# Attention of a two-layer decoder: causal masks added by matmuls, PSUM buffers divided anew, three value products split, divisions spread, late tokens first in the last head

## The chip, the cores and the metric

The kernel runs on one core of one Trainium2 chip. The metric is the device time of one execution in microseconds (us); the median of several runs counts. Engines are named as in the profile: PE is TensorE (PEld its weight loads), DVE is VectorE, ACT is ScalarE, POOL is GpSimd, SP is SyncE, whose queue issues most DMA transfers.

## The reference

A decoder trunk of two layers over 1024 tokens with 1024 features. Layer 0 is multi-head latent attention with 12 heads, layer 1 sliding-window attention; each has four memory cross-attention heads beside it, an output projection and a squared-ReLU MLP. The change is in layer 0's attention and in its output projection. Cut to what matters:

```python
def causal_dense_attention(q, k, v):          # q, k: 96 wide, v: 64 wide, 12 heads
    ...
        sc = jnp.einsum('bqhd,bkhd->bhqk', q_blk, k,
                        preferred_element_type=jnp.float32) * scale
        mask = k_idx[None, :] <= t_idx[:, None]
        sc = jnp.where(mask[None, None], sc, NEG)
        p = jax.nn.softmax(sc, axis=-1).astype(v.dtype)
        return jnp.einsum('bhqk,bkhd->bqhd', p, v)
...
        x = x + jnp.concatenate([mix, cross], axis=-1) @ w_o[i]
```

Inputs and output are float32.

## The kernel before

**Number format.** Most products are made from split operands: a float32 value is copied by ScalarE into a rounded part `hi` (type fp32r) and VectorE subtracts to get `lo`. A product then takes three matmul passes: hi·hi, hi·lo, lo·hi (`mm3`, L97). A product of unsplit float32 operands is one call, and the profile shows it as two matmul records (x2). The profile prints fp32r operands of matmuls as f32.

**Scores and row maxima.** For each head, `head_tiles` (L678) brings the head's queries and keys together by four DMAs, and splits them: ScalarE makes `qh` and `kh`, GpSimd subtracts for `ql` and `kl`. The softmax needs each query's largest score. `row_max(h, i)` (L707) makes the rough scores of query tile i against all keys up to its own tile (one pass, hi·hi) in a two-bank PSUM buffer (`ps2`, psx). VectorE then reduces the columns ahead of the diagonal tile (L718), and a second VectorE instruction adds the causal mask `dmask` to the diagonal 128 columns and takes the maximum (L719). `max_row` (L694) transposes the eight maxima and writes them, split, as row 96 of `qh` and `ql`, so that the score matmuls subtract them.

`scores(h, G, k)` (L815) makes transposed scores: keys of tile k on the partitions, queries of half G (512 tokens) on the columns, three passes over 97 rows into a one-bank buffer (`ps1`, pss). On the diagonal (k >= 4G) only the columns from the diagonal on are made (512, 384, 256 or 128), and VectorE adds `dmaskT` to the first 128 columns (L825). ScalarE takes the exponential into `p` (L827). For the early half (G = 0) `p` is split into `ph` and `pl`; the blocks of G = 1 stay whole (`WHOLE`).

**Values.** `values(h, G, k)` (L836) adds a block to the output pso of that half: one unsplit product of `vf` and `p` for G = 1 (L846), three passes for G = 0 (L849, L850 with 64 columns of weights, L854; that of the first block is issued last, L856). The weights have 64 columns of ones beside the 64 of v, so rows 64 to 127 hold the softmax denominators.

**Order.** The 12 blocks of a head are walked in the fixed list `blocks`, alternating the halves; step n issues the scores of block n and the values of block n - 2 (`LV = 2`). The row maxima of the next head are put between them by the table `ahead`, and `v_tiles` and `head_tiles` at steps 6 and 2 of a head. The framework then plans each engine's instruction order from this written order, its priorities and its own estimate of times, so an instruction can run ahead of its written place: the first split of w_o, written at step 4 of head 10, runs in the trace at 431.78 us, in head 9.

**Divisions.** Of heads 0 to 10 the undivided output goes by DMA into `qn`, and the denominators into `den`. `rc_split(c)` takes the reciprocals of a batch of heads (6 and 5), splits them and puts them in two rows per head by DMA; `rc_mul(c)` (L886) spreads each over 64 partitions by two matmuls of 6 or 5 rows with the selector `sel` (psrc, L894 and L895), and VectorE multiplies `qn` with it (L897). A batch's `rc_mul` is issued in one piece. The last head is divided directly: reciprocal of 64 x 512 (L859) and a product (L861) for each half.

**PSUM.** One pool for the whole kernel: two buffers of two banks (tag s) and four of one bank (tag m).

**Output projection.** `wo_phase` (L1015) goes over the eight token tiles twice, once for each half of w_o's columns, in the order `TORD` = 0, 4, 1, 5, 2, 6, 3, 7. Each tile's attention output is split by `o_split` (part 0 is `f0`, heads 0 to 7; part 1 is `f1`, heads 8 to 11 and the cross heads), and 24 matmuls follow (pswo).

Of the kernel before, what the change touches and what calls it, by code (L numbers as in the profile page):

```python
# [55 lines left out]
def trunk(  # L56
# [19 lines left out]
    ps_pool = pool("psum", space=PSUM)  # L76
    dram = ctx.enter_context(tc.tile_pool(name="dram", bufs=1, space=DRAM))

    def ps2(name):
        return ps_pool.tile([P, 1024], F32, tag="s", bufs=2, name=name)  # L80

    def ps1(name):
        return ps_pool.tile([P, 512], F32, tag="m", bufs=4, name=name)
# [34 lines left out]
    dmask = const.tile([P, P], F32, name="dmask")  # L118
    nc.gpsimd.memset(dmask, 0.0)
    nc.gpsimd.affine_select(out=dmask, in_=dmask, compare_op=ALU.is_ge, fill=NEG, base=0, pattern=[[-1, P]], channel_multiplier=1)  # L120
    dmaskT = const.tile([P, P], F32, name="dmaskT")
    nc.gpsimd.memset(dmaskT, 0.0)
    nc.gpsimd.affine_select(out=dmaskT, in_=dmaskT, compare_op=ALU.is_ge, fill=NEG, base=0, pattern=[[1, P]], channel_multiplier=-1)
# [342 lines left out]
    rope_tables()  # L466
    mem_kv(0, kv0, memT, pm)
# [239 lines left out]
    def row_max(h, i):  # L707
        if h not in m8s:
            m8s[h] = hb.tile([P, NT], F32, tag="m8", bufs=2, name=f"m8_{h}")
        qh, ql, kh, kl = bufs_[h % 3]  # L710
        n = (i + 1) * P
        ps = ps2(f"psx{h}_{i}")
        for a in range(0, n, 512):
            b = min(a + 512, n)
            nc.tensor.matmul(ps[:, a:b], qh[0:96, i * P : (i + 1) * P], kh[0:96, a:b], start=True, stop=True)  # L715
        m = m8s[h][:, i : i + 1]
        if i:
            nc.vector.reduce_max(m, ps[:, : n - P], axis=AX, negate=True)  # L718
        nc.vector.tensor_tensor_reduce(ps[:, n - P : n], ps[:, n - P : n], dmask, -1.0, m if i else -NEG, ALU.add, ALU.min, accum_out=m)  # L719
# [72 lines left out]

    at = pool("at", "right")
    for i in (1, 2):
        head_bufs(at, i)
# [16 lines left out]
    WHOLE = {(1, k) for k in range(8)}  # L812
    probs, po_ = {}, {}

    def scores(h, G, k):  # L815
        qh, ql, kh, kl = bufs_[h % 3]
        c0 = max(0, k - 4 * G) * P
        ks = slice(k * P, (k + 1) * P)
        qs = slice(G * 512 + c0, G * 512 + 512)
        ps = ps1(f"pss{h}_{G}_{k}")[:, c0:]  # L820
        nc.tensor.matmul(ps, kh[:, ks], qh[:, qs], start=True, stop=False)  # L821
        nc.tensor.matmul(ps, kh[:, ks], ql[:, qs], start=False, stop=False)
        nc.tensor.matmul(ps, kl[:, ks], qh[:, qs], start=False, stop=True)
        if k >= 4 * G:
            nc.vector.tensor_tensor(ps[:, 0:P], ps[:, 0:P], dmaskT, ALU.add)  # L825
        p = at.tile([P, 512], F32, tag="p", bufs=5, name=f"p{h}_{G}_{k}")
        nc.scalar.activation(p[:, c0:], ps, AF.Exp, scale=SC)  # L827
        if (G, k) in WHOLE:
            probs[(h, G, k)] = (p,)
            return  # L830
        ph = at.tile([P, 512], F32R, tag="ph", bufs=3, name=f"ph{h}_{G}_{k}")
        pl = at.tile([P, 512], F32R, tag="pl", bufs=3, name=f"pl{h}_{G}_{k}")
        split(p[:, c0:], ph[:, c0:], pl[:, c0:])
        probs[(h, G, k)] = (ph, pl)

    def values(h, G, k):  # L836
        vh, vl, vf = vbufs[h % 2]
        c0 = max(0, k - 4 * G) * P
# [5 lines left out]
        pr = probs.pop((h, G, k))  # L844
        if len(pr) == 1:
            nc.tensor.matmul(po[:, c0:], vf[:, k, :], pr[0][:, c0:], start=first, stop=last)  # L846
        else:
            ph, pl = pr
            nc.tensor.matmul(po[:, c0:], vh[:, k, :], ph[:, c0:], start=first, stop=False)  # L849
            nc.tensor.matmul(po[0:64, c0:], vl[:, k, :], ph[:, c0:], start=False, stop=False)  # L850
            if first and G == 0:
                probs["late"] = pl
            else:
                nc.tensor.matmul(po[:, c0:], vh[:, k, :], pl[:, c0:], start=False, stop=last and G == 1)  # L854
            if last and G == 0:
                nc.tensor.matmul(po, vh[:, 0, :], probs.pop("late"), start=False, stop=True)  # L856
        if last and h == H - 1:
            tmp = at.tile([64, 512], F32, tag="on", bufs=2, name=f"rq{h}_{G}")
            nc.vector.reciprocal(tmp, po[64:128])  # L859
            r = slice((h % 2) * 64, (h % 2) * 64 + 64)  # L860
            nc.vector.tensor_tensor(qn[h // 2][r, G * 512 : (G + 1) * 512], po[0:64], tmp, ALU.mult)  # L861
        elif last:
            on = at.tile([65, 512], F32, tag="on", bufs=2, name=f"on{h}_{G}")
            nc.scalar.activation(on, po[0:65], AF.Copy)
            r = slice((h % 2) * 64, (h % 2) * 64 + 64)
            nc.sync.dma_start(out=qn[h // 2][r, G * 512 : (G + 1) * 512], in_=on[0:64])
            d0 = (h % 6) * NT + 4 * G
            nc.sync.dma_start(out=den[h // 6][d0 : d0 + 4, :], in_=on[64:65])

    den = [at.tile([n, P], F32, name=f"den{n}") for n in (48, 40)]  # L870
# [3 lines left out]
    def rc_split(c):  # L874

        n = (6, 5)[c] * NT
# [9 lines left out]
    def rc_mul(c):  # L886
        rT = r_tiles.pop(c)
        n = (6, 5)[c]
        for s in halves:
            for j in range((n + 1) // 2):  # L890
# [5 lines left out]
                o = qn[3 * c + j][0 : 64 * m, s]  # L896
                nc.vector.tensor_tensor(o, pb, o, ALU.mult)  # L897

# [4 lines left out]
    seq = [(h,) + b for h in range(H) for b in blocks]  # L903

    ahead = {}
    for h in range(1, H):
        for i, d in ((7, -3), (6, -2), (5, -1), (4, 0), (3, 1), (2, 3), (1, 5), (0, 6), (8, 7)) if h > 1 else ((7, 3), (6, 4), (5, 5), (4, 6), (3, 7), (2, 8), (1, 9), (0, 9), (8, 10)):
            ahead.setdefault((h - 1) * len(blocks) + d, []).append((h, i))
    for n in range(len(seq) + LV):
        if n < len(seq):  # L910
            h, G, k = seq[n]
            j = n % len(blocks)
            scores(h, G, k)
            for g, i in ahead.get(n, ()):
                if i < NT:
                    row_max(g, i)
                else:
                    max_row(g)
            if h + 1 < H and j == 6:
                v_tiles(h + 1)  # L920
            if j == 2 and h + 2 < H:
                head_tiles(h + 2)
        if n >= LV:
            values(*seq[n - LV])
        if n >= 10 * len(blocks) and n % 2 == 0:
            wq.step()
        if n == 5 * len(blocks) + 3:
# [3 lines left out]
        if n == 5 * len(blocks) + 10:  # L931
            nc.scalar.activation(sel, sel32, AF.Copy)
        if n == 6 * len(blocks) + LV + 3:
            rc_split(0)
        if n == 7 * len(blocks) + LV:
            rc_mul(0)
        if n == 11 * len(blocks) + LV + 1:
            rc_split(1)
        if n == 11 * len(blocks) + LV + 8:
            rc_mul(1)  # L940
    at.release()
    hb.release()
# [72 lines left out]
    def wo_phase(layer, wq, o, m):  # L1015
# [12 lines left out]
        def o_split(t, parts_=(0, 1)):  # L1028
            r = []
            for i in parts_:  # L1030
                d = m.t(f"d{oct_[0] % 3}", F32R)
                oct_[0] += 1
                oh, ol = k4(d[:, 0, :]), k4(d[:, 1, :])
                split(o[i][:, :, t * P : (t + 1) * P], oh, ol)
                r += [(oh[:, k, :], ol[:, k, :]) for k in range(4)]
            return r

# [4 lines left out]

# [797 lines left out]
```

## Time and profile before

| | |
|---|---|
| median of 3 runs | 2184.77 us (2184.66 to 2185.63) |
| the profiled execution | 2188.77 us, its span 2187.1 us |
| mean granted TensorE clock | 0.988 |
| first score matmul of layer 0's attention | 254.38 us |
| third matmul of the output projection | 490.64 us |

The span is what the profile's times count in; the profiled execution's own time has 1.7 us around it. A row of the timeline gives start, duration, engine, line, operation, output <- inputs, and in brackets how long the engine was idle before and who released it. A row by windows gives the busy time of each engine with the number of instructions, then TensorE's granted clock (1.00 is full speed), the DMA engines' share and GB/s. A row by groups gives line, engine, operation, tiles and shapes, count | busy us, mean ns | idle before it and the releasers.

### The profile page before, as it was taken

How to read it: one execution, taken by the hardware profiler on the slowest of the kernel's cores; microseconds unless marked ns; L12 is line 12 of the kernel's file. 1: busy time of each engine (PE TensorE's matmuls, PEld its weight loads, DVE VectorE, ACT ScalarE, POOL GpSimd, SP SyncE). 2: the span in 40 equal slices, each digit the busy share in tenths (PEclk: the TensorE clock that was granted, in tenths of full speed). 3: DMA queues.
4: the chain of work that ended last, by engine and by line, in shares of the span. 5: the costliest groups of instructions: out<-in, count | busy, mean ns of one | idle time of the engine just before them, and what ended most of it. 6: DMA issues, size and time to landing. Idle time of an engine off the chain costs nothing.

```text
span 2187.1 us, 28756 instructions
## 1 busy us (share of the span) xinstructions
PE 2129.5 (97%) x9781; PEld 1715.1 (78%) x9781; DVE 1491.2 (68%) x3026; ACT 1000.9 (46%) x2119; POOL 234.4 (11%) x263
## 2 busy tenths in 40 slices
PE   6999999999999999999999999999999999999998
PEld 5888776658788888888888788668788888788887
DVE  6555677664997776786657443665987776785665
ACT  5455366544633333444445453774633333444452
POOL 0013433300000000000001133440000000000000
PEclk9999999899999999999999999999999999999999
DMA  7102222323254445953433111123254445854442
GB/s 245 59 11 59 52 69 46 80 88 121 83 173 150 140 141 175 342 198 125 164 118 99 63 39 49 39 76 108 78 175 148 159 158 176 319 189 139 131 121 87
DMA packets 171219, 272.97 MB, mean 125 GB/s; under 512 B 15699, under 2 KB 71744, under 8 KB 171072
## 3 DMA queue, kind: packets, MB, share of 16 engines
q1 hardware_dynamic: 164214, 253.80, 36.0%
q0 software_dynamic: 4016, 13.12, 1.6%
q10 hardware_dynamic: 2842, 4.22, 0.6%
q8 instruction: 77, 1.26, 0.2%
q14 instruction: 70, 0.57, 0.1%
HBM read 181.69 MB, written 76.81 MB: 118 GB/s over the span
## 4 chain that ended last, share of the span: by engine, by line
PE 87%; DVE 6%; ACT 2%; DMA 2%; issue 1%; POOL 1%; DVEq 0%; SPq 0%; ACTq 0%; POOLq 0%
PE psu L1214 5%; PE psu L1215 5%; PE psy L1501 5%; PE psy L1499 5%; PE psy L1500 5%; PE psu L1213 5%; PE psz L1499 4%; PE psz L1500 4%; PE psz L1501 4%; PE psv L1215 4%; PE psv L1214 4%; PE psv L1213 4%; PE pso L846 3%; PE pswo L102 2%; PE pswo L100 2%; PE pswo L101 2%
## 5 line engine op out<-in xcount | busy, mean ns | idle before, releaser
L91 ACT ACTIVATE i<-mr 128x512 fp32r<-128x512 f32 x78 | 49.3, 632 | 123.6 <-PE psu L1214 38.0
L827 ACT ACTIVATE p<-pss 128x512 f32<-128x512 f32 (+2 forms) x144 | 69.0, 484 | 77.4 <-DVE pss L825 55.7
L1499 PE MATMUL psy<-g 128*128 128x512 f32 x256 | 100.0, 391 | 0.0
L1500 PE MATMUL psy<-g 128*128 128x512 f32 x256 | 99.7, 390 | 0.0
L1501 PE MATMUL psy<-g 128*128 128x512 f32 x256 | 99.5, 390 | 0.0
L91 ACT ACTIVATE g<-i 128x512 fp32r<-128x512 f32 x79 | 49.7, 629 | 93.2 <-PE psz L1500 46.5
L846 PE MATMUL pso<-p,vf 128*128 128x512 f32 (+2 forms) x192 | 88.0, 542 | 0.7 <-ACT p L827 0.7
L92 DVE TENSOR_TENSOR g<-i,g 128x512 fp32r<-128x512 f32 x79 | 55.4, 702 | 45.9 <-ACT g L91 45.9
L821 PE MATMUL pss<-qh,kh 97*128 97x512 f32 (+2 forms) x144 | 77.8, 545 | 3.1 <-ACT p L827 2.5
L91 ACT ACTIVATE uh<-i 128x512 fp32r<-128x512 f32 x66 | 41.6, 630 | 83.5 <-PE psy L1500 40.7
L1499 PE MATMUL psz<-g 128*128 128x512 f32 x192 | 74.8, 389 | 0.0
L1501 PE MATMUL psz<-g 128*128 128x512 f32 x192 | 74.8, 389 | 0.0
L1500 PE MATMUL psz<-g 128*128 128x512 f32 x192 | 74.8, 389 | 0.0
L92 DVE TENSOR_TENSOR uh<-i,uh 128x512 fp32r<-128x512 f32 x66 | 45.6, 691 | 40.0 <-ACT uh L91 39.8
L718 DVE TENSOR_REDUCE m<-psx 128x1 f32<-128x128 f32 (+6 forms) x84 | 57.2, 686 | 20.7 <-PE psx L715 19.9
L92 DVE TENSOR_TENSOR i<-mr,i 128x512 fp32r<-128x512 f32 x78 | 53.8, 689 | 23.6 <-ACT i L91 23.4
L1424 DVE TENSOR_TENSOR mqf<-mqq,mqf 128x512 f32<-128x512 f32 x64 | 43.3, 690 | 28.8 <-DMA mqq<-in_mlp_w_down_dram 28.6
L1601 POOL TENSOR_TENSOR wsr<-wsr,gcol 128x1024 f32<-128x1024 f32 x12 | 23.7, 1979 | 352.7 <-DVE ul L1244 280.1
L91 ACT ACTIVATE i<-d 128x512 fp32r<-128x512 f32 x44 | 27.8, 633 | 70.2 <-PE psu L1214 39.6
L1501 PEld LDWEIGHTS psy<-g 128*128 128x128 f32 x256 | 48.1, 188 | 10.0
L1499 PEld LDWEIGHTS psy<-g 128*128 128x128 f32 x256 | 48.1, 188 | 9.8
L1500 PEld LDWEIGHTS psy<-g 128*128 128x128 f32 x256 | 48.1, 188 | 9.8
(610 smaller groups left out, 6942.2 us busy)
## 6 DMA issues: line engine op xcount, KB each, us to landing
i<-hd SPq DMA_DIRECT2D x154, 256.0 KB
hd<-uh SPq DMA_DIRECT2D x76, 256.0 KB
hd<-ul SPq DMA_DIRECT2D x76, 256.0 KB
mr<-in_mlp_w_up_dram SPq DMA_DIRECT2D x36, 512.0 KB
hd<-x SPq DMA_DIRECT2D x72, 256.0 KB
mr<-hd SPq DMA_DIRECT2D x70, 256.0 KB
d<-in_mlp_w_up_dram SPq DMA_DIRECT2D x32, 512.0 KB
mqq<-in_mlp_w_down_dram SPq DMA_DIRECT2D x32, 512.0 KB
```

The lines of the kernel that those rows point to most:

```text
L91: nc.scalar.activation(hi, src, AF.Copy)
L92: (lo_eng or nc.vector).tensor_tensor(lo, src, f32(hi), ALU.subtract)
L718: nc.vector.reduce_max(m, ps[:, : n - P], axis=AX, negate=True)
L821: nc.tensor.matmul(ps, kh[:, ks], qh[:, qs], start=True, stop=False)
L827: nc.scalar.activation(p[:, c0:], ps, AF.Exp, scale=SC)
L846: nc.tensor.matmul(po[:, c0:], vf[:, k, :], pr[0][:, c0:], start=first, stop=last)
L1213: nc.tensor.matmul(ps, wh[:, k, :], xh[:, k, :], start=p in (1, 2, 5) and k == 0, stop=False, skip_group_check=True)
L1214: nc.tensor.matmul(ps, wh[:, k, :], xl[:, k, :], start=False, stop=False, skip_group_check=True)
L1215: nc.tensor.matmul(ps, wl[:, k, :], xh[:, k, :], start=False, stop=k == 3, skip_group_check=True)
L1499: nc.tensor.matmul(ps, ah[:, j, :], bh, start=p in (1, 5, 2) and k == 0, stop=False, skip_group_check=True)
L1500: nc.tensor.matmul(ps, ah[:, j, :], bl, start=False, stop=False, skip_group_check=True)
L1501: nc.tensor.matmul(ps, al[:, j, :], bh, start=False, stop=k == NP - 1, skip_group_check=True)
```

## The change

1. *Masks.* An identity, `dmask` and `dmaskT` are bf16 tiles. The mask is added in PSUM by a matmul of the identity with the mask over the 128 diagonal columns, in `scores` after the first pass and in `row_max` as the last matmul. One reduction over all columns takes the row maximum.
2. *PSUM.* For the attention and the output projection of layer 0 the pool is released and made anew: six one-bank buffers and one two-bank buffer (tag x). Row maxima of tiles 0 to 3 use the former, of tiles 4 to 7 the latter. After the projection the old division returns.
3. *Value products.* (1, 1), (1, 2) and (1, 3) are split and take three passes; the early half's first block has its third pass in place. In the last head the early half stays whole.
4. *Order.* `scores` and `values` return lists of matmuls and a closure for what follows. Where either block is 128 columns wide, the two lists are issued alternately. The table `ahead` is shifted a little.
5. *Divisions.* Batches of 6, 4 and 1 heads; `rc_mul` is a generator that issues one pair of heads and one half in a step, late half first.
6. *Last head and projection.* The last head makes all late blocks and then the early ones; the late half is divided at once (`last_o(1)`), the early half inside the projection's second tile (`last_o(0)`). The projection's first pass goes over the tiles 4 to 7, then 0 to 3, with its split operands in the four x tiles; these lie where the key and query buffers of heads 10 and 11 were (pool hb1).

The core of the diff:

```diff
     def ps1(name):
-        return ps_pool.tile([P, 512], F32, tag="m", bufs=4, name=name)
+        return psum[0].tile([P, 512], F32, tag="m", bufs=4 if len(psum) == 1 else 6, name=name)
+    def psx(name):
+        return ps2(name) if len(psum) == 1 else psum[0].tile([P, 1024], F32, tag="x", bufs=1, name=name)
+    def new_psum(n):
+        psum[0].release()
+        psum[:] = [pool(f"psum{n}", space=PSUM)] * (2 if n == 1 else 1)
...
+    identb, dmask, dmaskT = [const.tile([P, P], BF16, name=n) for n in ("identb", "dmask", "dmaskT")]
+    def masks(pl):
+        nc.vector.tensor_copy(identb, ident)
+        for dst, sgn in ((dmask, 1), (dmaskT, -1)):
+            m = pl.tile([P, P], F32, tag="mask", bufs=2, name=f"mask{sgn}")
+            nc.gpsimd.memset(m, 0.0)
+            nc.gpsimd.affine_select(out=m, in_=m, compare_op=ALU.is_ge, fill=NEG, ...)
+            nc.vector.tensor_copy(dst, m)
...
     def row_max(h, i):
-        m = m8s[h][:, i : i + 1]
-        if i:
-            nc.vector.reduce_max(m, ps[:, : n - P], axis=AX, negate=True)
-        nc.vector.tensor_tensor_reduce(ps[:, n - P : n], ps[:, n - P : n], dmask, -1.0, m if i else -NEG, ALU.add, ALU.min, accum_out=m)
+        nc.tensor.matmul(ps[:, n - P : n], identb, dmask, start=False, stop=True, skip_group_check=True)
+        nc.vector.reduce_max(m8s[h][:, i : i + 1], ps[:, :n], axis=AX, negate=True)
...
+    blocks_end = [(1, k) for k in (0, 4, 5, 6, 7, 1, 2, 3)] + [(0, k) for k in range(4)]
-    WHOLE = {(1, k) for k in range(8)}
+    WHOLE = {(1, k) for k in (0, 4, 5, 6, 7)}
...
     def scores(h, G, k):
+        mms = [mm(ps, kh[:, ks], qh[:, qs], start=True, stop=False)]
+        if diag:
+            mms.append(mm(ps[:, 0:P], identb, dmaskT, start=False, stop=False))
+        mms.append(mm(ps, kh[:, ks], ql[:, qs], start=False, stop=False))
+        mms.append(mm(ps, kl[:, ks], qh[:, qs], start=False, stop=True))
...
-        if k >= 4 * G:
-            nc.vector.tensor_tensor(ps[:, 0:P], ps[:, 0:P], dmaskT, ALU.add)
...
+            if (G, k) in WHOLE or (h == H - 1 and G == 0):
+                probs[(h, G, k)] = (p,)
...
+    def last_o(G, tmp):
+        nc.vector.reciprocal(tmp, po_[G][64:128])
+        nc.vector.tensor_tensor(qn[5][64:128, G * 512 : (G + 1) * 512], po_[G][0:64], tmp, ALU.mult)
+    GRP = [0, 6, 10, 11]
...
     def rc_mul(c):
+        for s in halves[::-1]:
             for j in range((n + 1) // 2):
...
                 nc.vector.tensor_tensor(o, pb, o, ALU.mult)
+                yield
...
-        for i, d in ((7, -3), (6, -2), (5, -1), (4, 0), (3, 1), (2, 3), (1, 5), (0, 6), (8, 7)) if h > 1 else ...
+        for i, d in ((7, -4), (6, -2), (5, 0), (3, 1), (4, 2), (2, 3), (1, 5), (0, 6), (8, 7)) if h > 1 else ...
...
+        if ms and mv and P in (width(*seq[n][1:]), width(*seq[n - LV][1:])):
+            while ms and mv:
+                mix += [ms.pop(0), mv.pop(0)]
+        for f in mix + ms:
+            f()
...
+        next(muls, None)
...
+        if n == 7 * NB + LV:
+            muls = rc_mul(0)
+        if n == 10 * NB + LV + 1:
+            rc_split(1)
+        if n == 10 * NB + LV + 8:
+            muls = rc_mul(1)
+        if n == 11 * NB + LV + 1:
+            rc_split(2)
+        if n == 11 * NB + LV + 6:
+            muls = rc_mul(2)
...
     def wo_phase(layer, wq, o, m):
+        ORD = [[4, 5, 6, 7, 0, 1, 2, 3] if layer == 0 else TORD, TORD]
...
+                if p == 1 and layer == 0 and half == 0:
+                    last_o(0, m.t("i39")[0:64, 0, :])
```

199 lines of the change are left out of this document (111 added, 88 removed).

## The prediction

> **What bounds the kernel now.** First the page's busy line: TensorE is busy for 97% of the span, so only TensorE time counts, spent on matmuls, on waiting, or at a lowered clock.
>
> ```profile
> PE 2129.5 (97%) x9781; PEld 1715.1 (78%) x9781; DVE 1491.2 (68%) x3026; ACT 1000.9 (46%) x2119; POOL 234.4 (11%) x263
> ```
>
> The change touches only layer 0's attention and the start of its output projection. I cut that stretch at the first score matmul of each head (its start in the timeline), which gives heads 0 to 11, the last running to the output projection's third matmul, and a rest of 3.15 us. The columns are window, length, PE, PEld, DVE, ACT and POOL busy, granted clock, DMA.
>
> ```profile
> 254.38:278.33 23.95, 20.61 (x87) 14.68 (x87) 21.22 (x49) 13.12 (x25) 15.78 (x11) 0.93 0.29 65
> 278.33:293.42 15.09, 14.74 (x72) 10.99 (x71) 11.12 (x35) 10.38 (x21) 4.75 (x3) 1.00 0.39 84
> 293.42:310.13 16.71, 16.61 (x79) 12.29 (x78) 12.65 (x38) 11.22 (x23) 6.00 (x3) 1.00 0.27 64
> 310.13:326.86 16.73, 16.63 (x79) 12.28 (x78) 12.66 (x38) 11.12 (x23) 6.02 (x3) 1.00 0.27 64
> 326.86:343.57 16.71, 16.61 (x79) 12.28 (x78) 12.64 (x38) 11.15 (x23) 6.01 (x3) 1.00 0.29 64
> 343.57:362.26 18.69, 17.08 (x80) 12.13 (x78) 12.58 (x38) 11.26 (x24) 7.11 (x5) 1.00 0.26 57
> 362.26:379.23 16.97, 16.59 (x79) 12.25 (x78) 13.37 (x40) 11.07 (x24) 6.02 (x3) 1.00 0.09 21
> 379.23:407.52 28.29, 27.05 (x89) 17.59 (x88) 16.96 (x43) 10.82 (x22) 5.97 (x3) 0.78 0.24 58
> 407.52:427.67 20.15, 18.49 (x82) 12.73 (x80) 14.67 (x38) 10.84 (x23) 6.04 (x3) 0.97 0.29 65
> 427.67:446.08 18.41, 17.90 (x80) 12.35 (x78) 16.41 (x40) 14.26 (x26) 5.44 (x3) 1.00 0.50 153
> 446.08:461.50 15.42, 15.32 (x73) 11.25 (x72) 9.38 (x33) 8.57 (x19) 0.56 (x1) 1.00 0.19 52
> 461.50:490.64 29.14, 24.30 (x85) 13.78 (x83) 17.78 (x26) 11.95 (x24) 0.00 (x0) 0.88 0.29 91
> 490.64:493.79 3.15, 3.15 (x8) 2.48 (x8) 3.15 (x4) 0.00 (x0) 0.00 (x0) 0.50 0.02 5
> ```
>
> The reader is to see a steady head of 16.7 us with a full TensorE, and four places above it: head 0, heads 7 and 8, and the last head with what follows it. In the steady heads only TensorE work can be won or lost; in the other places there are waits and low clock.
>
> **TensorE's prices.** Matmuls overlap, so a price is the distance between starts, not the duration.
>
> ```profile
> 382.47 1.02 PE L846 MATMUL pso<-p,vf 128*128 128x512 f32 x2
> 382.93 0.80 PE L821 MATMUL pss<-qh,kh 97*128 97x512 f32 x1
> 383.57 0.40 PE L822 MATMUL pss<-ql,kh 97*128 97x512 f32 x1
> 383.80 0.39 PE L823 MATMUL pss<-qh,kl 97*128 97x512 f32 x1
> 384.04 1.02 PE L846 MATMUL pso<-p,vf 128*128 128x512 f32 x2
> ...
> 322.07 0.28 PE L822 MATMUL pss<-ql,kh 97*128 97x128 f32 x1
> 322.18 0.28 PE L823 MATMUL pss<-qh,kl 97*128 97x128 f32 x1
> ...
> 323.57 0.22 PE L850 MATMUL pso<-ph,vl 128*64 128x128 f32 x1
> 323.63 0.27 PE L854 MATMUL pso<-pl,vh 128*128 128x128 f32 x1
> ```
>
> A split-pass matmul of 512 columns costs 0.23 (383.57 to 383.80); 384 and 256 columns cost in proportion 0.175 and 0.115. From one whole value product to the next (382.47 to 384.04) is 1.57 with three such score matmuls between, so the whole product costs 1.57 - 0.69 = 0.88. A 128-column matmul between full-width weights costs 0.11 (322.07 to 322.18), only 0.06 where the weights have 64 columns (323.57 to 323.63).
>
> A steady head has 27 split matmuls of 512, counting scores, row maxima and values, and 11 each of 384, 256 and 128: 6.2 + 1.9 + 1.3 + 1.2, plus whole products 5 x 0.88 + 0.66 + 0.44 + 0.22 = 5.7, plus 0.1 for the transpose: 16.4. So 0.3 of the 16.7 is waiting.
>
> **The change, part by part.**
>
> *Masks on TensorE.* Per head 16 added 128-column bf16 matmuls (8 diagonal score blocks, 8 row maxima), 192 in all. The trace has no bf16 matmul. Nearest rows: 0.06 below, 0.11 as usual, and 0.22 above, if the identity's weights and those of the next matmul are both uncovered. A gain is excluded, since TensorE must execute them. I take 0.11, because the matmul behind each mask loads full-width weights, as at 322.18: +1.76 a head, 21.1 in all (11.5 to 42).
> [...]
>
> What leaves VectorE for this:
>
> ```profile
> L825 DVE TENSOR_TENSOR pss<-pss,dmaskT 128x128 f32<-128x128 f32 x96 | 28.4, 297 | 23.8 <-PE pss L823 19.7 <-ACT ph L91 1.6 <-PE psx L715 1.1
> L719 DVE CUSTOM_DVE_ANT_0 psx<-psx,dmask,m 128x128 f32<-128x128 f32 x78 | 27.3, 356 | 2.0
> L92 DVE TENSOR_TENSOR pl<-p,ph 128x512 fp32r<-128x512 f32 x12 | 10.2, 850 | 3.3 <-ACT ph L91 2.8
> L718 DVE TENSOR_REDUCE m<-psx 128x1 f32<-128x896 f32 x12 | 13.1, 1088 | 10.1 <-PE psx L715 10.1
> L91 ACT ACTIVATE ph<-p 128x512 fp32r<-128x512 f32 x12 | 7.5, 628 | 0.2
> ```
>
> Per head 8 x 0.30 + 8 x 0.36 = 5.3 goes. At most 8 x 0.30 = 2.4 comes back, since each reduction reads 128 more columns, and three subtractions of up to 0.85 come: VectorE stays at or below its 12.7. ScalarE gains three copies of 0.63 and goes from 11.1 to 13.0. Neither becomes the bound. The exponential no longer waits for VectorE, worth nothing by itself in a full head.
>
> *Three value products in split passes.* 0.88 becomes 0.69, 36 times: -6.8, or -0.57 a head. The last head's early group does the reverse, with 1280 columns whole: 2.2 against 1.75, +0.45.
>
> *PSUM.* The six one-bank buffers take the 0.3 of waiting; I count -0.2 a head. Added wait: the wide row maxima share one two-bank buffer, so the next one's matmuls, and the values and scores queued behind them on TensorE, wait for VectorE's reduction. They stand two steps (2.8 us) apart and a reduction of 896 columns takes 1.1: taken as 0, and 1.1 each without that cover. The PSUM division's two borders and the masks made later (three small VectorE copies before TensorE starts): 0, at most 1.
> A steady head becomes 16.4 - 0.57 + 1.76 + 0.1 = 17.7: 1.0 *longer*.
>
> *Interleaving narrow matmuls* of scores and values: 0, since each still has the next weights behind it; at best the 0.05 between the two narrow prices for about 12 matmuls a head.
>
> *Divisions spread.* Head 7 issues its 12 division matmuls, which have only 6 rows, nearly together.
>
> ```profile
> 388.00:394.00 6.00, 6.00 (x14) 3.37 (x13) 2.66 (x7) 0.93 (x2) 0.00 (x0) 0.51 0.30 79
> 403.00:407.00 4.00, 4.00 (x12) 3.27 (x11) 2.19 (x5) 1.86 (x5) 3.60 (x2) 0.50 0.49 108
> ...
> 387.52 0.49 PE L894 MATMUL psrc<-rTq,sel 6*128 6x512 f32 x1
> 388.18 2.08 PE L846 MATMUL pso<-p,vf 128*128 128x512 f32 x2
> ```
>
> The clock is halved right behind the burst (the whole product at 388.18 takes 2.08 instead of 1.02) though TensorE shows no gap there, and again at 403: 10 us at half clock, 5 lost. The rest is VectorE's multiplications holding score buffers. Spread over steps, the matmuls cost their 12 x 0.23 = 2.8 and no more. Heads 7 and 8: 2 x 17.7 + 2.8 + 0.5 = 38.7 against 48.4, -9.7. The second batch moves 8 matmuls (1.8) into head 10, and 4 (0.9) stay in head 11; the third batch adds a reciprocal, a split and two transfers on SP's queue, off the path.
>
> *Late tokens first.*
>
> ```profile
> 490.64 0.79 PE L102 MATMUL pswo<-woq,d 128*128 128x512 f32 x1 [4.04 <-DVE d L92]
> 485.78 3.36 DVE L859 RECIPROCAL rq<-pso 64x512 f32<-64x512 f32 x1 [3.72 <-PE pso L846]
> 489.18 0.68 DVE L861 TENSOR_TENSOR fa<-pso,rq 64x512 f32<-64x512 f32 x1
> 489.89 0.69 DVE L92 TENSOR_TENSOR d<-qn,d 128x512 fp32r<-128x512 f32 x1
> ```
>
> Now VectorE's chain of 3.36 + 0.68 + 0.69 stands bare behind the last value product. Afterwards the early group's products, about 2.8 us, cover it, so about 2 stays bare. The other reciprocal and product (4.0) go into the projection's second tile, where VectorE has two subtractions and an addition of 0.69 in 24 x 0.23 = 5.6 us; the tiles behind have slack too: 0, or up to 4 if not covered.
> Head 11 with its rest (32.3 now): scores 6.6 and masks 0.9, late group 5.7 - 0.57, early group 2.2, divisions 0.9, the ten projection matmuls inside it 2.3, gap 2, waits 0.8: 20.8, -11.5.
>
> *Other heads.* Heads 2 to 4: +2.9. Head 5 keeps its wait of 1.5 (the row below) and what follows it: +0.9. Head 6: +0.7. Head 9, where w_o's splits stand: +0.3. Head 10 (without two of the next head's row maxima, with the second divisions): 18.4, +3.0. Head 0's own row maxima, made before it: 8 masks, +0.9. Heads 0 and 1 take 39.0 for 34.0 of work (three steady-type row maxima more than two heads have); head 0's row shows the cause, VectorE busy for 21.2 of 23.95 and a clock of 0.93.
>
> ```profile
> 350.90 0.44 PE L821 MATMUL pss<-qh,kh 97*128 97x384 f32 x1 [1.49 <-ACT p L827]
> ```
>
> I take half of the excess of 5 as gone: 36.6 + 2.5 = 39.1, +0.1.
>
> Sum: -9.7 - 11.5 + 2.9 + 0.9 + 0.7 + 0.3 + 3.0 + 0.9 + 0.1 = -12.4 us. The profiled execution took 2188.77 (span 2187.1 and 1.7 around it), 4.0 above the median of the runs; it would become 2176.4, and the median 2184.77 becomes 2172.4.
>
> **The rivals.**
>
> 1. *Cheap masks:* 0.06 each. For it: the 64-column row, and bf16 weights are half as large. 9.6 less: 2162.8.
>
> 2. *The half clock stays:* spread low-row matmuls still bring it, at the same 5 us: 2177.4. For it: TensorE waited for nothing at 388, so what the clock answers to is not settled by this trace. Against: the steady heads, in which narrow matmuls stand between wide ones, all have 1.00.
>
> 3. *Slower: VectorE locked by GpSimd.* The three new subtractions read two SBUF operands while GpSimd splits the coming head's keys and queries:
>
> ```profile
> 413.64 2.39 POOL L92 TENSOR_TENSOR ql<-q,qh 96x1024 fp32r<-96x1024 f32 x1 [6.74 <-PE pss L823]
> 414.11 2.47 DVE L92 TENSOR_TENSOR pl<-p,ph 128x512 fp32r<-128x512 f32 x1
> 315.37 0.68 DVE L92 TENSOR_TENSOR pl<-p,ph 128x512 fp32r<-128x512 f32 x1
> ```
>
> The same subtraction takes 0.68 alone and 2.47 when GpSimd is inside its own, ending just behind it. Head 11's products aside, 11 heads could lose 1.8 each in the value product that needs the low part: +20, 2192. It decides from 1.1 a head. Against: the last block's low part is needed two steps (about 3 us) after its scores, and the steady heads' four subtractions now avoid the collision. The half-way case, 0.8 a head, gives 2181.
> [...]
>
> 4. *Dear masks:* 0.22 each: +21, 2193.5. Against: wide matmuls stand ahead of most masks and cover the identity's load.
>
> **How the numbers follow.** Forecast 0.50; cheap masks 0.15; half clock stays 0.10; lock half-way 0.13; lock in full 0.07; dear masks 0.05. About 0.2% (4.4 us) is what a measurement can tell from no change. Faster: forecast, cheap masks, half clock, 0.75. Same: half-way lock, 0.13. Slower: 0.12. The forecast's own range is 2166 to 2179 (gap of the tail and excess of heads 0 and 1, some 3 each way, masks by 0.02 either way). With cheap masks and less waiting below (2159) and the half-way lock with an uncovered reciprocal above (2185), all but about 0.15 is held.
>
> **What will show it.** Steady heads of 17.7 with 16 bf16 matmuls each, 0.11 behind one another; masks at 0.06 would give 16.9. Heads 7 and 8 below 20 with clock 1.00. A gap of 2 us or less ahead of the first projection matmuls. Subtractions over 1.5 us with TensorE waiting for them would show rival 3. The order on each engine is planned anew for the whole stage, so a split or reciprocal put in another place than the written one is what could make this wrong.

## The result, and the profile after

The changed kernel takes 2218.24 us in the median (2217.61 to 2218.95) against 2184.72 us (2184.27 to 2185.63) for the kernel before: a ratio of 1.0153, 95% interval 1.0135 to 1.0171. It is slower by 33.5 us, where 12.4 us less was predicted, and lies outside the range of 2159 to 2185. The profiled executions differ by 29.0 us in span (2216.1 and 2187.1), and the comparison below is made between these two; the one of the kernel before stands 4.0 us above its median, that of the changed kernel 0.7.

The page's busy line of the changed kernel: TensorE is still busy for 97% of a longer span.

```profile
PE 2151.1 (97%) x10005; PEld 1717.9 (78%) x10005; DVE 1486.9 (67%) x2789; ACT 1018.5 (46%) x2154; POOL 235.1 (11%) x263
```

The heads of the changed kernel by windows, cut as in the prediction; the last window runs to the tenth matmul of the output projection (518.5). Columns: window, length, PE, PEld, DVE, ACT and POOL busy, granted clock, DMA.

```profile
251.30:279.10 27.80, 21.83 (x108) 14.16 (x109) 23.54 (x24) 14.73 (x27) 15.89 (x10) 0.99 0.26 58
279.10:297.50 18.40, 18.40 (x86) 12.78 (x85) 8.39 (x14) 10.68 (x22) 3.65 (x2) 0.84 0.30 65
297.50:320.70 23.20, 21.36 (x97) 13.85 (x96) 13.56 (x18) 12.45 (x26) 6.02 (x3) 0.85 0.19 46
320.70:341.50 20.80, 18.38 (x97) 12.38 (x96) 13.52 (x18) 12.37 (x26) 6.05 (x3) 1.00 0.23 52
341.50:364.90 23.40, 21.30 (x97) 13.80 (x96) 13.64 (x18) 12.54 (x26) 6.01 (x3) 0.85 0.20 45
364.90:385.70 20.80, 18.43 (x98) 12.42 (x97) 13.54 (x18) 12.77 (x27) 6.98 (x5) 1.00 0.24 53
385.70:409.10 23.40, 21.13 (x97) 13.89 (x96) 14.60 (x20) 12.60 (x28) 6.03 (x3) 0.85 0.06 15
409.10:432.20 23.10, 23.10 (x103) 14.68 (x102) 12.84 (x22) 10.49 (x23) 1.28 (x1) 0.93 0.19 47
432.20:455.90 23.70, 21.55 (x104) 14.43 (x103) 13.74 (x19) 15.18 (x29) 10.69 (x5) 0.93 0.31 70
455.90:477.00 21.10, 20.26 (x97) 13.69 (x96) 16.26 (x23) 16.06 (x30) 6.03 (x3) 0.92 0.46 133
477.00:495.00 18.00, 18.00 (x94) 12.09 (x92) 8.64 (x16) 11.56 (x26) 1.28 (x1) 1.00 0.21 66
495.00:518.50 23.50, 23.37 (x98) 14.11 (x98) 14.50 (x19) 11.65 (x26) 0.00 (x0) 1.00 0.37 115
```

| part | before | predicted | after | missed by |
|---|---|---|---|---|
| heads 0 and 1 | 39.0 | 39.1 | 46.2 | 7.1 |
| heads 2 to 6 | 85.8 | 90.3 | 111.6 | 21.3 |
| heads 7 and 8 | 48.5 | 38.7 | 46.8 | 8.1 |
| head 9 | 18.4 | 18.7 | 21.1 | 2.4 |
| head 10 | 15.4 | 18.4 | 18.0 | -0.4 |
| head 11 to the tenth projection matmul | 32.3 | 20.8 | 23.5 | 2.7 |

The rest of the difference is small: the first score matmul stands 3.1 us earlier, the way from the projection's tenth matmul to the MLP's first is 3.3 us longer, what follows 1.0 longer. With the heads' 27.8 that is the 29.0. (In the experiments below the first score matmul stands anywhere from 250.3 to 254.8 us, so the 3.1 is put down to no part of the change.)

The steady heads, predicted at 17.7, take 20.8 and 23.4. In each TensorE waits for 1.8 to 2.4 us (length less busy time); in every second one the clock falls to 0.85. The list of TensorE's waits from 250 to 530 us, first rows (engine, tile, line, what was waited for: us in total, times, longest):

```profile
PE pso L879 <- DVE pl L100: 16.2, 14, 2.0
PE psx L729 <- ACT kh L99: 2.1, 1, 2.1
PE psx L729 <- DVE m L731: 1.0, 2, 0.7
```

One wait carries nearly all: the third pass of a split value product waits for VectorE's subtraction that makes the low part `pl`. The timeline of head 4 shows why, TensorE's rows first, then VectorE's, then GpSimd's:

```profile
344.97 0.50 PE L879 MATMUL pso<-pl,vh 128*128 128x512 f32 x1 [1.62 <-DVE pl L100]
347.91 0.80 PE L879 MATMUL pso<-pl,vh 128*128 128x512 f32 x1 [0.48 <-DVE pl L100]
...
340.39 0.69 DVE L100 TENSOR_TENSOR pl<-p,ph 128x512 fp32r<-128x512 f32 x1 [0.63 <-ACT ph L99]
342.46 2.46 DVE L100 TENSOR_TENSOR pl<-p,ph 128x512 fp32r<-128x512 f32 x1 [0.38 <-ACT ph L99]
344.84 0.94 DVE L731 TENSOR_REDUCE m<-psx 128x1 f32<-128x768 f32 x1
345.71 2.15 DVE L100 TENSOR_TENSOR pl<-p,ph 128x512 fp32r<-128x512 f32 x1
...
341.99 2.38 POOL L100 TENSOR_TENSOR kl<-k,kh 96x1024 fp32r<-96x1024 f32 x1 [10.86 <-ACT kh L99]
344.93 2.37 POOL L100 TENSOR_TENSOR ql<-q,qh 96x1024 fp32r<-96x1024 f32 x1 [0.57 <-ACT qh L99]
```

The subtraction of 0.69 us becomes 2.46 and 2.15 exactly where GpSimd subtracts the next head's keys and queries: it ends 0.55 behind GpSimd both times, so by an estimate from these rows 0.55 of the 0.69 that it takes alone is done after GpSimd has finished. The reduction at 344.84, whose input lies in PSUM and which also runs beside GpSimd, keeps its length: 0.94, and 0.95 at 410.87, where GpSimd is idle. Why the one is held up and the other not is shown by no run. The two blocks struck are (1, 2) and (1, 3), two of the three that the change splits: they close a head, their subtractions are due at the opening of the next, and there GpSimd's work falls. In the kernel before, GpSimd stood at the same place, 0.3 us behind the start of head 4 (326.86):

```profile
327.15 2.38 POOL L92 TENSOR_TENSOR kl<-k,kh 96x1024 fp32r<-96x1024 f32 x1 [0.46 <-DMA den<-on]
329.49 2.38 POOL L92 TENSOR_TENSOR ql<-q,qh 96x1024 fp32r<-96x1024 f32 x1
```

### The profile page after: what moved, and what is told of

Its sections match the earlier page's. It is cut to its first block, busy times and chain, and to the rows that moved or that the text cites. A ratio compares the mean times of both kernels' runs of the same rounds, so it can differ in the third digit from the quotient of the medians.

```text
span 2216.1 us, 28995 instructions
## 1 busy us (share of the span) xinstructions
PE 2151.1 (97%) x10005; PEld 1717.9 (78%) x10005; DVE 1486.9 (67%) x2789; ACT 1018.5 (46%) x2154; POOL 235.1 (11%) x263
## 4 chain that ended last, share of the span: by engine, by line
PE 88%; DVE 5%; ACT 3%; DMA 1%; issue 1%; POOL 0%; SPq 0%; DVEq 0%; ACTq 0%; POOLq 0%
PE psu L1306 5%; PE psu L1307 5%; PE psu L1305 5%; PE psy L1591 5%; PE psy L1593 5%; PE psy L1592 5%; PE psz L1591 4%; PE psz L1593 4%; PE psz L1592 4%; PE psv L1305 4%; PE psv L1306 4%; PE psv L1307 4%; PE pss L845 4%; PE pso L879 3%; PE pswo L110 3%; PE pswo L108 3%
## 5 line engine op out<-in xcount | busy, mean ns | idle before, releaser
L731 DVE TENSOR_REDUCE m<-psx 128x1 f32<-128x640 f32 (+7 forms) x96 | 72.3, 754 | 43.9 <-PE psx L730 42.7
L100 DVE TENSOR_TENSOR pl<-p,ph 128x512 fp32r<-128x512 f32 (+3 forms) x80 | 73.1, 917 | 30.3 <-ACT ph L99 30.2
L99 ACT ACTIVATE g<-i 128x512 fp32r<-128x512 f32 x79 | 49.7, 629 | 93.2 <-PE psz L1592 46.2
L845 PE MATMUL pss<-qh,kh 97*128 97x512 f32 (+2 forms) x144 | 68.4, 478 | 0.6 <-DMA qh<-mhl 0.6
L845 PE MATMUL pss<-ql,kh 97*128 97x512 f32 (+2 forms) x144 | 60.5, 420 | 0.0
L99 ACT ACTIVATE i<-d 128x512 fp32r<-128x512 f32 x44 | 27.8, 633 | 70.0 <-PE psu L1306 39.6
L1593 PEld LDWEIGHTS psy<-g 128*128 128x128 f32 x256 | 48.0, 188 | 10.0
L1592 PEld LDWEIGHTS psy<-g 128*128 128x128 f32 x256 | 48.1, 188 | 9.9
```

Source lines behind the costliest of these rows:

```text
L99: nc.scalar.activation(hi, src, AF.Copy)
L100: (lo_eng or nc.vector).tensor_tensor(lo, src, f32(hi), ALU.subtract)
L731: nc.vector.reduce_max(m8s[h][:, i : i + 1], ps[:, :n], axis=AX, negate=True)
L845: return lambda: nc.tensor.matmul(o, a, b, skip_group_check=True, **kw)
L1592: nc.tensor.matmul(ps, ah[:, j, :], bl, start=False, stop=False, skip_group_check=True)
L1593: nc.tensor.matmul(ps, al[:, j, :], bh, start=False, stop=k == NP - 1, skip_group_check=True)
```

## The experiments

All ratios are to the kernel before, with 95% intervals.

**1. The splits undone in the changed kernel.**

```diff
-    WHOLE = {(1, k) for k in (0, 4, 5, 6, 7)}
+    WHOLE = {(1, k) for k in range(8)}
```

> The changed kernel with all late blocks whole again (the three split value products undone, nothing else). Theory L (the subtractions of the three new splits are held up by GpSimd's subtractions for keys and queries, TensorE waits for them 2 to 2.4 us in each head, and the gaps bring the half clock, some 2.5 us in every second head): both go, heads of about 18.2 instead of 20.8 and 23.3, and the time falls by 30 to 45 us to about 2182 (2173 to 2188). Theory M (the masks on TensorE or the shared two-bank buffer for row maxima are what makes heads long): the whole products cost 0.2 each more and the time rises by about 6, to 2225.

Measured: 2197.53 us, 1.0059 (1.0044 to 1.0074). The three splits cost 20.7 us of the 33.5, less than the lock theory expected; the waits for `pl` in the steady heads are gone, the clock there is 1.00, and they take 18.3. Something else costs too.

**2. The splits kept, and the key and query subtractions moved from GpSimd to VectorE.**

```diff
-        split(q32, qh[0:96], ql[0:96], lo_eng=nc.gpsimd)
-        split(k32, kh[0:96], kl[0:96], lo_eng=nc.gpsimd)
+        split(q32, qh[0:96], ql[0:96])
+        split(k32, kh[0:96], kl[0:96])
```

> The changed kernel with the subtractions of the key and query splits on VectorE instead of GpSimd; the three new splits stay. Theory L: nothing on GpSimd is left for the new subtractions to collide with except the short one for the values, VectorE pays about 2.4 us a head of which it has room, and the time falls to about 2178 (2168 to 2190). Theory C (the chain exponential, copy, subtraction is too long for two steps, whoever does the other subtractions): TensorE still waits for the low parts, and the time stays above 2205.

Measured: 2187.78 us, 1.0011 (1.0002 to 1.0020): 30 us below the changed kernel with the same split products. A steady head by windows, and VectorE's timeline at the opening of the next:

```profile
310.70:328.50 17.80, 17.80 (x98) 12.50 (x97) 12.74 (x20) 12.32 (x26) 2.03 (x1) 1.00 0.27 60
...
328.94 1.21 DVE L100 TENSOR_TENSOR kl<-k,kh 96x1024 fp32r<-96x1024 f32 x1
330.08 0.68 DVE L100 TENSOR_TENSOR pl<-p,ph 128x512 fp32r<-128x512 f32 x1
331.55 0.68 DVE L100 TENSOR_TENSOR pl<-p,ph 128x512 fp32r<-128x512 f32 x1
```

Up to 382 us every 512-column subtraction is back at 0.68 or 0.69 (a few of the later ones take 1.3 to 1.4), TensorE is busy for the whole 17.8 (its bf16 mask matmuls included), and the half clock has left the steady heads with the waits. 17.8 is the steady head that the prediction worked out (17.7). The cause of the greater part is thereby shown: not the passes, but the meeting of two engines' subtractions. GpSimd gave up two subtractions of 2.38 us a head, which cost VectorE 1.21 each.

**3. The splits alone, in the kernel before.**

```diff
-    WHOLE = {(1, k) for k in range(8)}
+    WHOLE = {(1, k) for k in (0, 4, 5, 6, 7)}
```

> The kernel before with only the three value products split. Theory L: the same waits of TensorE for the low part come in here, 2 us or more a head and the half clock in some, and the 0.6 saved a head does not pay for them: about 2220 (2200 to 2245). Theory M: without masks on TensorE the splits give their 6 us: about 2179.

Measured: 2213.55 us, 1.0134 (1.0119 to 1.0149). One line of the change, without any other, makes the kernel 28 us slower, with the same mark on VectorE and a wait of 1.4 us for it in each of heads 2 to 6:

```profile
322.02 1.97 DVE L92 TENSOR_TENSOR pl<-p,ph 128x512 fp32r<-128x512 f32 x1
326.17 0.69 DVE L92 TENSOR_TENSOR pl<-p,ph 128x512 fp32r<-128x512 f32 x1 [0.56 <-ACT ph L91]
```

**4. Whole products, and the masks back on VectorE.** Experiment 1 with the masks as in the kernel before; what is left of the change is PSUM, order, divisions and the tail.

```diff
-        nc.tensor.matmul(ps[:, n - P : n], identb, dmask, start=False, stop=True, skip_group_check=True)
-        nc.vector.reduce_max(m8s[h][:, i : i + 1], ps[:, :n], axis=AX, negate=True)
+        ...   # the lines of before, and dmaskT added by VectorE
```

> The changed kernel with the late blocks whole and the masks added by VectorE as before; the PSUM division, the interleaving, the spread divisions and the late tokens first stay. Against the run with whole blocks alone this gives the price of 192 mask matmuls: at 0.11 to 0.12 us each 21 to 23 us, less the waits for VectorE that come back (up to 5). Expected 2164 (2156 to 2174), which would beat the kernel before by what the divisions and the late tokens gain (about 19 us). If masks are cheap (0.05 and less), it is within 8 us of the run with whole blocks.

Measured: 2186.87 us, 1.0004 (0.9992 to 1.0017). The masks cost 10.7 us net by the medians (12 by the ratios); the expected 2164 was missed, so the rest of the change brings nothing. Heads 6 to 9 by windows:

```profile
362.60:379.80 17.20, 17.08 (x80) 12.37 (x78) 13.54 (x39) 11.10 (x24) 6.03 (x4) 1.00 0.09 21
379.80:400.40 20.60, 20.60 (x87) 13.10 (x86) 13.34 (x39) 8.90 (x20) 0.80 (x2) 1.00 0.17 42
400.40:428.80 28.40, 24.00 (x84) 16.77 (x82) 18.35 (x43) 13.31 (x27) 11.72 (x6) 0.77 0.35 78
428.80:450.00 21.20, 19.88 (x80) 13.55 (x78) 16.83 (x41) 14.33 (x26) 5.96 (x3) 0.90 0.43 136
```

Spreading the division matmuls does free head 7 of the half clock (28.3 at a mean clock of 0.78 before, 20.6 at 1.00 now), but head 8 takes it over (28.4 at 0.77). Its beginning, in TensorE's, SP's queue's and GpSimd's rows:

```profile
396.85 0.39 PE L935 MATMUL psrc<-rTk,sel 6*128 6x512 f32 x1
404.80 0.96 PE L723 MATMUL psx<-kh,qh 96*128 96x512 f32 x3 [1.63 <-ACT kh L99]
...
397.04 0.51 SPq L690 DMA_DIRECT2D q<-fa  x1
398.28 0.54 SPq L692 DMA_DIRECT2D k<-kq  x1
...
402.02 2.34 POOL L100 TENSOR_TENSOR ql<-q,qh 96x1024 fp32r<-96x1024 f32 x1 [0.64 <-ACT qh L99]
404.83 2.40 POOL L100 TENSOR_TENSOR kl<-k,kh 96x1024 fp32r<-96x1024 f32 x1 [0.47 <-ACT kh L99]
```

Head 9's queries are loaded right behind the last division matmul. In `rc_split` the reciprocals' tiles take the tags `q32` and `k32`, the single slots into which `head_tiles` loads: spread over six steps, the divisions hold the next head's load back. In the kernel before, the last division matmul stands at 390.78 and the key load at 392.2, here at 396.85 and 398.28.

**5. The divisions in one go again**, in the kernel of experiment 4.

```diff
-            muls = rc_mul(0)
+            for _ in rc_mul(0): pass      # also for batches 1 and 2
```

> The kernel with whole value products and VectorE masks (2186.9) with each batch of division matmuls issued in one go again, at the step at which it now begins. Theory R: the slots come free some 6 us earlier, head 9's keys are not waited for, and head 8 is back at about 20; whether head 7 goes back to 28 says what the burst by itself does to the clock. If the burst brings the half clock: heads 7 and 8 take 28 + 20 as before the change, 2186 to 2188. If it doesn't: 20 + 20, 2178. Under theory N (low-row matmuls bring the half clock wherever they stand): head 7 at 28 and head 8 at 20.

Measured: 2180.12 us, 0.9972 (0.9962 to 0.9982). Heads 7 and 8 take 27.7 with clock 0.75 and 18.9 with clock 1.00: with the burst the half clock is back in head 7 (0.50 from 386 to 392, with TensorE busy all the time), and head 8 is free of the wait for the key split (0.45 us of it is left, in head 7). Neither outcome that I had priced (2186 to 2188 or 2178) is met exactly: the two heads go from 49.0 to 46.6, and heads 9 to 11 win 5.6 more.

**6. The division matmuls earlier, still spread**, in the kernel of experiment 4. (The more direct test, tiles of their own for the reciprocals, was expected at 2177 but doesn't fit: it needs 60.5 kb a partition where 52.8 are left.)

```diff
-        if n == 6 * NB + LV + 3:
+        if n == 6 * NB + LV + 1:
             rc_split(0)
-        if n == 7 * NB + LV:
+        if n == 6 * NB + LV + 5:
             muls = rc_mul(0)
```

> The kernel with whole value products and VectorE masks (2186.9) with one edit: the first batch of reciprocals is split two steps earlier and its division matmuls, still one step apart, begin seven steps earlier (in head 6 instead of head 7), so that the last of them stands two steps before head 9's loads need the shared slots. Theory R (shared slots): no wait on ScalarE's key split, GpSimd's splits of heads 9 and 10 again apart, no half clock: heads 6, 7 and 8 together 53 to 56 instead of 66.1, whole kernel 2176 (2173 to 2179). Theory N (the low-row matmuls, or head 8's own load): a half clock of some 5 us stays in one of the three heads, 2184 to 2188.

Measured: 2181.18 us, 0.9983 (0.9973 to 0.9992). The wait for the key split is gone, and heads 6, 7, 8 and 9 take 22.8 (clock 0.92), 19.1, 19.6 and 17.9 against 17.2, 20.6, 28.4 and 21.2. The shared slots are thereby shown as the reason for head 8's 28.4. The gain of 5.7 us (4.6 by the ratios) is half of what I had expected: heads 6 to 8 take 61.5 instead of 53 to 56. Head 6 pays for the matmuls, and part of what theory N named is there as well, a clock of 0.68 from 381 to 385.

**7. As 6, with the later batches in one go.**

> As the run before, with the second and third batch (heads 10 and 11) in one go. In the kernel with all batches in one go, heads 9 to the tenth projection matmul took 56.4 against 62.0 when spread, without a half clock. If that is due to these two batches: 5 below the run before, 2171 (2167 to 2175), and below both kernels. If it came from the first batch's earlier release (head 9's 3 us): no more than 2 below it.

Measured: 2181.93 us, 0.9992 (0.9979 to 1.0006): nothing won, so the 5.6 us in heads 9 to 11 of experiment 5 didn't come from these two batches alone; where they came from stays open.

**8. The old division of PSUM**, in the kernel of experiment 7: both calls of `new_psum` removed.

> As the second run of this call, with the old division of PSUM all through (four one-bank and two two-bank buffers, wide and narrow row maxima in the two-bank ones). If the new division helps as I put it (0.2 a head): 2 to 3 slower than that run. If its border ahead of the MLP costs the wait for ScalarE's last copies (2.2 to 3.3 in the traces that have it): 0 to 2 faster, and that wait gone. If buffers bound the narrow blocks: waits for exponentials and maxima in each head, 5 to 10 slower.

Measured: 2185.69 us, 1.0007 (0.9994 to 1.0021), 3.8 above the run before by the medians, with overlapping intervals. Its steady head takes 17.0 against 16.6, its head 6 31.3 with clock 0.73, and the wait ahead of the MLP is gone, as expected. The new division is worth 0.4 a steady head in these traces, and its border costs 2.2 to 3.3 us where the wait shows. The profiled execution stands 7.5 us above the median of this kernel, and head 6, with the same spread matmuls as in experiment 7, is at clock 0.50 from 385 to 401, so its 31.3 isn't put down to PSUM.

**9. The old end of the attention**, in the kernel of experiment 4: `blocks` for the last head too, the early half split and divided there, the projection's tiles in the old order.

> The kernel with whole value products and VectorE masks (2186.9) with the old end of the attention: the last head's blocks in the usual order, both halves divided there, the early half of the last head in split products, the projection's tiles in the old order with the old split buffers. Theory T (the tail saves what the trace of the last head shows, 32.3 against 23.9): 8 us slower, 2195 (2192 to 2198), with the wait of about 4 us ahead of the first projection matmuls back. Rival: what the tail saves ahead of the projection is lost behind it: 2187 to 2189.

Measured: 2190.93 us, 1.0026 (1.0016 to 1.0035): late tokens first saves 4 to 5 us, half of what the trace of before suggested. Its last head takes 28.4 (32.3 before the change), with the wait in front of the projection back:

```profile
488.58 0.80 PE L110 MATMUL pswo<-woq,d 128*128 128x512 f32 x1 [4.43 <-DVE d L100]
```

**10. The masks alone, in the kernel before**, in the score blocks (shown) and in `row_max` as in the change.

```diff
+            nc.tensor.matmul(ps[:, 0:P], identb, dmaskT, start=False, stop=False, **kw)
-            nc.vector.tensor_tensor(ps[:, 0:P], ps[:, 0:P], dmaskT, ALU.add)
```

> The kernel before with the masks alone moved to TensorE (bf16 identity, one reduction for each row maximum); everything else as before. Theory G (the full gross price): 192 matmuls of 0.11 make each steady head 1.7 longer, 18.4; with nothing won in the places with waits 2206 (2203 to 2209). Theory H (part is won back because VectorE has 4 us less a head): the waits for VectorE in heads 0, 8 and 11 shrink and the net is 8 to 14, 2194 to 2200. If the masks were near free: 2186.

Measured: 2200.08 us, 1.0066 (1.0054 to 1.0078): 14.5 us slower. A steady head by windows, and two masks among TensorE's rows:

```profile
311.60:329.90 18.30, 18.30 (x95) 12.28 (x94) 8.62 (x15) 11.03 (x23) 5.99 (x3) 1.00 0.25 59
...
313.56 0.79 PE L826 MATMUL pss<-qh,kh 97*128 97x512 f32 x1
314.19 0.23 PE L828 MATMUL pss<-dmaskT,identb 128*128 128x128 bf16 x1
314.24 0.47 PE L829 MATMUL pss<-ql,kh 97*128 97x512 f32 x1
314.55 0.40 PE L830 MATMUL pss<-qh,kl 97*128 97x512 f32 x1
```

From 314.19 to 314.55 is 0.36 for a mask and a pass that costs 0.23: 0.13. The head is 1.6 longer for its 16 masks, 0.10 each. VectorE drops from 12.7 to 8.6 and gives TensorE nothing for it in this head, which had no wait to lose.

**11. VectorE with both loads**: experiment 2 with the masks back on VectorE.

> The changed kernel with the key and query subtractions on VectorE (2187.8) and the masks back on VectorE as well; the split value products stay. TensorE would need 17.8 - 1.7 = 16.1 a head, VectorE 12.75 + 5.3 - 1.7 = 16.4. If VectorE can run full: heads of 16.4 to 16.8, about 12 x 1.2 = 14 less, 2174 (2171 to 2179). If VectorE as the bound makes TensorE wait (low parts, score blocks and row maxima late): heads of 17.5 to 20 with gaps for VectorE, 2185 to 2200. Heads 8 and 9 should keep the wait for ScalarE's key split.

Measured: 2192.51 us, 1.0027 (1.0015 to 1.0038). A steady head by windows:

```profile
308.20:325.90 17.70, 16.94 (x81) 12.60 (x80) 15.51 (x44) 12.16 (x26) 1.30 (x1) 1.00 0.26 61
```

17.7 instead of 16.4 to 16.8: VectorE is at 15.5 us, TensorE is busy for 16.9 and waits in small pieces. With the three splits' subtractions and those of keys and queries VectorE can't take the masks as well without making TensorE wait, though it isn't full itself.

**12. The best version**: whole products, masks on VectorE, early division matmuls (experiment 6), key and query subtractions on VectorE.

> The best kernel so far that has the early division matmuls (2181.2) with the key and query subtractions moved from GpSimd to VectorE. If what is left of the lock can still be won: no subtraction of a low part over 1 us, the waits of 0.9 and 1.8 for it in head 8 gone, VectorE at 12.6 + 2.4 = 15.0 of 16.6 us a steady head, whole kernel 2178 (2175 to 2180). If the fuller VectorE makes exponentials, row maxima or divisions late: steady heads over 16.8 and 2182 to 2188.

Measured: 2174.50 us (2173.64 to 2176.11), 0.9954 (0.9940 to 0.9968): 10 us faster than the kernel before and 44 faster than the changed one.

```profile
310.90:327.30 16.40, 16.40 (x80) 12.26 (x78) 13.89 (x39) 10.79 (x23) 1.24 (x2) 1.00 0.29 66
380.20:399.70 19.50, 18.80 (x82) 12.91 (x82) 14.97 (x39) 11.12 (x22) 1.27 (x1) 1.00 0.30 69
399.70:417.20 17.50, 17.18 (x78) 12.13 (x77) 14.04 (x40) 10.54 (x22) 0.68 (x1) 1.00 0.38 84
```

The steady head and heads 7 and 8: 16.4 is the work that the prediction counted for the head before, with nothing left of waiting; heads 7 and 8 take 37.0 (head 6, which now has the division matmuls, 20.0), and no clock but head 1's (0.91) is below 1.00.

## Why the prediction was wrong

**The step that failed is the weight of rival 3.** The mechanism was named, with its price (1.8 a head), the row that shows it (2.47 against 0.68) and the point from which it decides (1.1 a head); it was given 0.07 in full and 0.13 half-way, and in the sum it stood at nothing. The reason against it was that the last block's low part is needed two steps later, and that the four subtractions of before avoid the collision. Those four belong to early blocks; the new three close a head, and GpSimd's two subtractions of 2.38 run at the opening of the next head in the trace. GpSimd's rows of the trace before (327.15 and 329.49), laid beside the places of blocks (1, 1) to (1, 3), already say so. In the sum the subtractions stood as VectorE's busy time alone ("Neither becomes the bound"), which was true and beside the point: it is busy for 13.5 of 20.8 us in such a head. The price came out at 3.0 a head instead of 1.8 (20.8 against 17.8 in experiment 2, about 2.2 of it plain waiting in heads 2 to 6), because two of the three are struck; behind the waits the clock falls in every second steady head, which costs about 2.6 more there (23.4 against 20.8) and which the rival's price didn't hold. That is the 21.3 of heads 2 to 6: measured between the transposes of the maxima, these five heads take 111.6 in the changed kernel and 89.3 in experiment 2, for a predicted 90.3. It is about half of the 7.1 of heads 0 and 1 (experiment 2 is 3.8 shorter from the first score matmul to the transpose of head 2's maxima); most of the other half should be the old excess there, of which the sum took 2.5 as gone. That part is argued.

The lock alone doesn't save the forecast: without it, in experiment 2, the kernel takes 2187.8, 15 above the 2172.4 and still outside the range. The divisions and the tail below hold most of that.

**Masks at 0.11: right as a price** (0.10 to 0.13 in experiment 10). 14.5 net alone, 10.7 in company, where 21.1 was counted: VectorE's relief is felt in heads with waits, such as head 8 (19.3 in experiment 10, 20.2 before).

**Splits at -0.57 a head: right as TensorE work.** With the lock gone the steady head is 17.8, for 17.7, and 0.5 shorter than with whole products (18.3 in experiment 1).

**Divisions spread, -9.7: missed by 8.1.** The step that failed is that spread matmuls "cost their 12 x 0.23 = 2.8 and no more". The prediction left out that their tiles share the loading slots, so that a later last matmul is a later load; in the changed kernel too, head 8 waits 2.15 us for the key split. The matmuls' own clock effect was read rightly only in part: spread, head 7 keeps 1.00 in experiment 4, and in one go it falls to 0.75; but in the changed kernel itself the spread matmuls end at 427.1 and the clock is 0.63 from 429 to 433, with TensorE busy all the time since 409. That is rival 2, which comes in some runs and not in others (see the last section).

**Tail, -11.5: 8.8 in the trace, 4 to 5 as an edit of its own.** The bare wait of 4 us did go, and so did the 2.8 of gap and waits that the sum kept; the work was counted 5.4 too low, 18.0 for 23.4. By the distances between the starts, scores and masks take 8.6 (7.5 in the sum), values 9.1 (7.3), division matmuls 3.2 (0.9) and the projection 2.6 (2.3). Six of the eight division matmuls that the sum put into head 10 stand here, so head 10's 18.0 for 18.4 is luck in part. As for the 4 to 5: with the old end the last head takes 28.4 instead of 32.3, so some 4 us of the gain come without the tail. Before, the clock was 0.50 from 481 to 486.5, behind the 12 division matmuls of this head (474.9 to 480.7); in experiment 9 it is 1.00 from 480 to 484. That the moved divisions are the reason is argued.

**PSUM: -0.2 a head was 0.4, and its border was taken as 0, at most 1.** In the changed kernel the MLP's first matmul waits until ScalarE has emptied the old division's last buffers:

```profile
615.78 0.50 PE L1305 MATMUL psu<-mqq,uh 128*128 128x512 f32 x1 [3.29 <-ACT x L1160]
```

With the old division all through (experiment 8) this wait is gone. It is also missing in experiments 4, 9 and 11, which have the border, so the border alone doesn't bring it.

**The sum of the parts.** Undone one after the other from the changed kernel, splits 20.7, masks 10.7 and all the rest 2.2 (2186.87 against 2184.72) make the 33.5; by the ratios they are 20.5, 12.0 and 0.9. Alone in the kernel before, splits and masks cost 28 and 14.5, more than together: with the masks off VectorE, its queue behind a locked subtraction is shorter. In experiment 3 TensorE also waits 7.6 us for row maxima, in the changed kernel 1.0, which agrees; but that last reason is argued and not shown.

## What to carry to other kernels

Before work is given to VectorE, lay the new instructions' places beside GpSimd's rows: VectorE, at two thirds of its time (67%), was late at the one moment that counted, and moving GpSimd's subtractions to VectorE paid although VectorE got busier (12.6 to 13.9 us a steady head from experiment 6 to 12, 6.7 us won). When a step is spread or moved, ask which buffers it holds for longer and who loads into them. Work moved onto the engine that is busy all the time must bring back more than its price there; 16 small matmuls a head did not (1.6 us more a steady head and 14.5 us more in all in experiment 10).

## What the hardware showed that I had not expected

**The half clock.** In the changed kernel heads 2, 4 and 6 have 0.85 and heads 3 and 5 have 1.00, with nearly the same waits (1.6 us each, and a second of up to 0.8). Head 4 by stretches of 4 us:

```profile
342.00:346.00 4.00, 2.38 (x12) 1.27 (x11) 3.62 (x4) 2.85 (x5) 3.43 (x2) 1.00 0.13 29
346.00:350.00 4.00, 3.52 (x11) 1.76 (x10) 2.57 (x3) 1.71 (x3) 1.31 (x1) 0.58 0.28 70
350.00:354.00 4.00, 4.00 (x13) 2.26 (x12) 1.40 (x2) 1.33 (x3) 1.26 (x1) 0.57 0.61 132
354.00:358.00 4.00, 4.00 (x25) 2.85 (x24) 1.90 (x4) 2.09 (x5) 0.00 (x0) 1.00 0.00 0
```

The clock falls behind a stretch in which TensorE was busy for 2.38 of 4 us. These waits are at most 1.63 us, and nearly the same ones leave the clock at 1.00 in the next head; no run shows why. Behind a longer wait it was halved too: in experiment 9 the clock is 1.00 from 480 to 484 and 0.50 behind the wait of 4.43 us, from 488.6 to 492.5.

It also comes without such a wait, at the 12 division matmuls of 6 rows. In one go they are followed by 0.50 in experiment 5 (388 to 392). Spread over 10 to 20 us, they have 0.63 right behind them in the changed kernel (429 to 433) and 0.60 in experiment 1 (406 to 410), and 0.68 and 0.50 among them in experiments 6 (381 to 385) and 8 (385 to 401); in the changed kernel TensorE had then been busy without a break since 401 or earlier, in experiments 6 and 8 since 372.2 and 376.5. In experiments 2, 4, 7, 9, 11 and 12 the clock stays at 1.00 through the same 12 matmuls and for 3 us behind them, and experiments 6 and 7 have the same first batch. So spreading makes the half clock rarer at best, and what exactly the clock answers to stays open.

**Prices.** The subtraction of 96 x 1024 takes 2.38 us on GpSimd (341.99 in the changed kernel) and 1.21 on VectorE (328.94 in experiment 2).
